# Sixteen DRAM copies of broadcast rows, a landing margin for more of a hand-written schedule, and two more products of ones

## The chip, the cores and the metric

The kernel runs on one core of a Trainium2 chip. Its time is the device time of one execution in microseconds (us), the median over the runs shown. The engines of the core are named as in the profile: PE is TensorE (PEld its weight loads), DVE is VectorE, ACT is ScalarE, POOL is GpSimd, SP is SyncE, which here issues nearly all of the DMAs. 16 DMA engines carry the transfers.

## The reference

One layer of a decoder trunk on 1024 tokens of 2048 channels, then a final RMSNorm, all in float32:

```python
h = rmsnorm(x, ln_g)
proj = h @ w_in                      # split into gMLP, DeltaNet and cross-attention columns
out_a = gmlp_spatial_gating(g_u, g_v, ws, bs, ln_g, ln_b) * silu(g_z)     # chunks of 128 tokens
q, k, v = split(silu(causal_conv(d_q, d_k, d_v)))                         # 8 heads of 128
g = -exp(a_log) * softplus(d_a + dt_bias); beta = sigmoid(d_b)            # decay and step per token and head
o = gated_delta_rule(l2norm(q), l2norm(k), v, g, beta)                    # chunks of 64 tokens, a scan over them
out_b = rmsnorm(o, dn_norm_g) * silu(d_z)
mk, mv = split(rmsnorm(mem, mem_norm_g) @ w_mem_kv)                       # 256 memory tokens
out_c = softmax(c_q @ mk.T / sqrt(128)) @ mv * silu(c_z)                  # 4 heads of 128
y = rmsnorm(x + concat(out_a, out_b, out_c) @ w_out, final_g)
```

Two things of it matter below. The vector `ln_g` (2048 values) multiplies every row of `x`, and so has to stand on all 128 partitions. The decays of a head, summed up over a chunk (a row of 512 values for each head and half of the tokens), have to stand on all partitions too, where the matrix of decays is made from them.

## The kernel before, in words

**Products.** Every large product is done as three products of float32 values that are split into a high and a low part (`whi`, `wlo` for weights, `ahi`, `alo` or `gt`, `inv` for the left side): ACT copies the high part, DVE subtracts it from the raw value. PE takes high x high, high x low and low x high into a PSUM bank (`acc` for the main sums, `dn` for the rest). The large projections go by a scheme with seven products of half blocks.

**The order of the work.** The program doesn't issue instructions as it states them. A class `Plan` records every operation with its engine, its dependencies and a rank (`rank(2)` around a block of the code: smaller goes first), gives it a cost, and then plays the program through: on each engine the next operation is the one of the smallest rank among those that are ready. When all have a planned start, they are sorted by it and issued, all from line 297, which is why the profile shows the one line L297 for everything and tells groups apart by tile names. No engine waits for the plan itself; only the order of each engine's instructions comes from it. When the plan decides at what time a successor `s` of a finished operation is ready, it adds a margin `s.late` to the end of a DMA (`o.moves`), or to the end of another engine's work that PE reads:

```python
o.late = self.slow if eng == "pe" else self.late if self.cls > self.URGENT else 0.0
...
if o.moves or s.eng == "pe" != e:
    when += s.late
```

So an operation that isn't PE's and has a rank above 2 is planned `late` nanoseconds after a load that it reads has landed. `late` is 0 until line 1235, which stands behind the first stage, and 1000 from there on. PE's own margin `slow` is 0 but for the two-head solves inside `levels` (800 there). The margin is in the plan alone: no instruction of the chip waits for it.

**The first stage.** PE starts with seven products of a matrix of ones with itself, `warm(7)` (each float32 product shows as two records), which go to a spare `dn` bank and are read by nobody. Then it transposes the first 512 columns of the 256 memory rows (`spread_mem(0)`, tiles `kT` and `qT` into `gt` and `inv`), and a loop over 16 steps `k` multiplies the 128 weight rows of step `k` (`load_kv`, tiles `ut` for the first four and `wraw`, loaded by SP) with the memory columns. The high part of the weights, `whi<-ut,gcol` or `whi<-wraw,gcol`, is made on ACT, which multiplies by the norm's weight on the way. In between stand the other column blocks of the memory (`spread_mem`) and the first token tiles of `x`: `load_x` brings 128 tokens in four blocks of 512 columns (tile `vs` for the first tile of tokens, `kd` for the second), `prep` squares them on ACT (`jk<-kd`), multiplies each by its scale and by `ln_g` on DVE, lets PE transpose the block into a spare bank and ACT empty that bank (`tn<-dn`). Each of these spare banks is one of two that take turns.

`ln_g` comes into four `zg` tiles, one for each 512 columns, each 128 partitions x 512 values. At step 3 of the loop SP issues four loads, and every one of them reads a single row of 2 KB in DRAM 128 times:

```python
if k == 3:
    with rank(2), behind(kvmark[-1]):
        for c in range(4):
            Q.dma_start(gb[c], ln_g[0, c * HT : (c + 1) * HT].partition_broadcast(P))
```

**The decays.** `decays` (line 785) makes the summed decays of one half of the tokens for all heads, transposes them into a tile `gr` of 64 rows x 128 and stores it to a DRAM tensor `gcd` of 8 heads x 512 (line 835). For each head and half, `qk` (line 922) loads the head's row on all partitions into a tile `E` through POOL's queue (line 936), again one row of 2 KB read 128 times, 16 loads in all. ACT makes exponentials of it.

**The later stages** are the projections, the two-head solves and scans of the gated delta rule (`front`, `inverse`, `levels`, `back`), the gating by chunks, the attention and the output projection. Most loaded tiles are split or copied by ACT and DVE before PE sees them. In a few places PE reads a loaded tile itself: the blocks of the two-head solves, the transposes of the first stage, and `gmlp` (line 1605), where SP loads `vd` into a tile `el` and PE multiplies it with `wsT`.

Of the kernel before, what the change touches and what calls it, by code (L numbers as in the profile page):

```python
# [17 lines left out]
P = 128  # L18
D = 2048
# [3 lines left out]
HT = 512  # L23
# [22 lines left out]

class Op:
    __slots__ = ("eng", "fn", "args", "kw", "cls", "idx", "cost", "lat", "moves", "lock", "n", "succ", "ready", "at",
                 "lead", "tail", "table", "late")


class Engine:
# [8 lines left out]
class Plan:  # L61
# [7 lines left out]
    TABLES = {AF.Exp: "exp", AF.Silu: "silu", AF.Gelu_apprx_tanh: "gelu"}  # L69
    TABLE_LOAD = 1500.0  # L70
    STAY = 1.5
    URGENT, LATE = 2.0, 1000.0

    def __init__(self, nc):
        self.ops = []
        self.seen = {}
        self.heir = {}
        self.users = {}
        self.cls = 5.0
        self.gate = None  # L80
        self.bundle = None
        self.late = self.slow = 0.0
        self.pe = Engine(self, "pe", nc.tensor)
        self.act = Engine(self, "act", nc.scalar)
        self.dve = Engine(self, "dve", nc.vector)
        self.pool = Engine(self, "pool", nc.gpsimd)
        self.sp = Engine(self, "sp", nc.sync)
# [50 lines left out]
    def add(self, eng, name, fn, args, kw):  # L138
        o = Op()
        o.eng, o.fn, o.args, o.kw, o.cls, o.idx = eng, fn, args, kw, self.cls, len(self.ops)  # L140
        o.succ, o.n, o.ready = [], 0, 0.0
        o.table = self.TABLES.get(args[2]) if eng == "act" and len(args) > 2 else None
        outs, ins = [], []
        for i, a in enumerate(args):
            if hasattr(a, "tensor"):
                (outs if i == 0 else ins).append(a)
        for key, a in kw.items():
            if hasattr(a, "tensor"):
                (outs if key in ("out", "accum_out") else ins).append(a)
        self.price(o, name, outs, ins)  # L150
        deps = set()
        if self.gate is not None:
            deps.add(self.gate)
        for write, aps in ((False, ins), (True, outs)):
            for ap in aps:
                key, p0, p1, mask = self.region(ap)
                log = self.seen.setdefault(key, [])
                keep = []
                for e in log:
                    q0, q1, m, w, op = e  # L160
                    if p0 < q1 and q0 < p1 and mask & m:
                        if (write or w) and op is not o:
                            deps.add(op)
                        if write and p0 <= q0 and q1 <= p1 and not m & ~mask:
                            continue
                    keep.append(e)
                keep.append((p0, p1, mask, write, o))
                self.seen[key] = keep
                if key in self.users:
                    self.users[key].append(o)  # L170
                    if write:
                        deps.update(self.users.get(self.heir.get(key), ()))
        o.lead, o.tail = o, []
        o.late = self.slow if eng == "pe" else self.late if self.cls > self.URGENT else 0.0
        if eng == "pe" and self.bundle is not None:
            if self.bundle:
                o.lead = self.bundle[0]
                o.lead.tail.append(o)
            self.bundle.append(o)
        for d in deps:  # L180
            if d.lead is not o.lead and o.lead not in d.succ:
                d.succ.append(o.lead)
                o.lead.n += 1
        self.ops.append(o)
        return o
# [42 lines left out]
    def issue(self):  # L228
        free = dict.fromkeys(self.SEEN, 0.0)
        soon = {e: [] for e in free}  # L230
        now = {e: [] for e in free}
        held = {"dve": 0.0, "pool": 0.0}
        dma = 0.0
        beside = dict.fromkeys(free, 0.0)
        table = "exp"
        for o in self.ops:
            if o.n == 0 and o.lead is o:
                heapq.heappush(soon[o.eng], (0.0, o.idx))
        left = len(self.ops)
        while left:  # L240
            best = None
            for e in free:
                if now[e]:
                    t = free[e]
                elif soon[e]:
                    t = max(free[e], soon[e][0][0])
                else:
                    continue
                if best is None or t < best[0]:
                    best = (t, e)  # L250
            t, e = best
            while soon[e] and soon[e][0][0] <= t:
                i = heapq.heappop(soon[e])[1]
                heapq.heappush(now[e], (self.ops[i].cls, i))
            if e == "act":
                other = [(c + self.STAY * (self.ops[i].table not in (None, table)), i, c) for c, i in now[e]]
                _, i, c = min(other)
                now[e].remove((c, i))
                heapq.heapify(now[e])
                head = self.ops[i]  # L260
            else:
                head = self.ops[heapq.heappop(now[e])[1]]
            for o in (head, *head.tail):
                t = max(t, free[e])
                if o.table not in (None, table):
                    t, table = t + self.TABLE_LOAD, o.table
                o.at = t
                left -= 1
                if o.lock:
                    t = max(t, held["pool" if e == "dve" else "dve"])  # L270
                end = t + o.cost
                if o.lock:
                    held[e] = end
                free[e] = end - min(self.OVERLAP[e], 0.5 * o.cost)
                done = end + o.lat
                if o.moves:
                    dma = max(dma, end) + o.moves
                    beside[e] = max(beside[e], end) + 2 * o.moves
                    done = (dma if e == "sp" else beside[e]) + self.DMA_FIXED + o.lat
                for s in o.succ:  # L280
                    if s.eng != e or o.moves:
                        when = done + self.SEEN[s.eng] + (self.SLACK if s.eng == "pe" else 0.0)
                    elif e == "pe":
                        when = free[e]
                    else:
                        when = end + 34.0
                    if o.moves or s.eng == "pe" != e:
                        when += s.late
                    s.ready = max(s.ready, when)
                    s.n -= 1  # L290
                    if s.n == 0:
                        heapq.heappush(soon[s.eng], (s.ready, s.idx))
            if len(head.tail) > 7:
                free[e] += self.SWITCH
        self.ops.sort(key=lambda o: (o.at, o.idx))
        for o in self.ops:
            o.fn(*o.args, **o.kw)  # L297
# [3 lines left out]
def kernel(  # L301
# [28 lines left out]
    R = Plan(nc)  # L330
# [90 lines left out]
    def tpb():  # L421
        turn["tp"] += 1
        return acc[2 + turn["tp"] % 2]

    h0_d = DT([KT, P, HT], "h0d")
    hT_d = DT([KT, P, HT], "hTd")

# [57 lines left out]
    def row_tiles(tag):  # L485
        if tag in ("inv", "gt", "ut"):
            return [b[:, i * HT : (i + 1) * HT] for b in (ring[tag](), ring[tag]()) for i in range(2)]
        return [ring[tag]() for _ in range(4)]

    gb = [ring["zg"]() for _ in range(4)]  # L490
    kvraw += [ring["ut"]() for _ in range(2)]
    mem_rows = [row_tiles("kT"), row_tiles("qT")]
# [20 lines left out]
    y1 = C([P, 2 * NT, 32], "y1")  # L513
    rows = y1.rearrange("p c m -> p (c m)")[:, 0:P]
    mrow = rows[0:16]
    with rank(2):
        load_mem(0)
        S.dma_start(mrow, mem_norm_g[0].rearrange("(c p) -> c p", p=P))
        for k in range(4):
            load_kv(k)  # L520
            if k == 1:
                load_mem(1)
    with rank(3):
        load_mem(2)
        load_mem(3)
# [66 lines left out]
    rm = []  # L592
    kvmark = []
    mhl = [spread_mem(0)]
    for k in range(KT):
        mh, ml = mhl[k // 4]
        if k >= 4:
# [16 lines left out]
        if k == 3:  # L614
            with rank(2), behind(kvmark[-1]):
                for c in range(4):
                    Q.dma_start(gb[c], ln_g[0, c * HT : (c + 1) * HT].partition_broadcast(P))
        if k in (1, 4, 8):
            with behind(kvmark[-1]):
                mhl.append(spread_mem(len(mhl)))  # L620
# [153 lines left out]
    r3, ww = ([steps[:, i * P : (i + 1) * P] for i in two] for two in ((0, 1), (2, 3)))  # L774
    scs = [C([P, 7, NT, NH], f"sc{hf}") for hf in range(2)]
    sct = C([P, 5, NT, NH], "sct")
    gcs = [DT([NH, HT], f"gcd{hf}") for hf in range(2)]
    scan_banks, work = dnr.bufs[0:2], over(dnr.bufs[2:4])

    def decay_mm(a, k):  # L780
# [4 lines left out]
    def decays(hf, a):  # L785
# [12 lines left out]
        with rank(1):  # L798
# [33 lines left out]
            V.tensor_copy(byh.rearrange("p (h t) -> p t h", t=NT), dp[:, 0:NU].rearrange("p (t h) -> p t h", h=NH))  # L832
            PE.transpose(tp[0:NU, 0:P], byh, ident)
            V.tensor_copy(gr, tp[0:NU, 0:P])
            Q.dma_start(gcs[hf].rearrange("h (t p) -> (h t) p", p=P), gr)


    todo = []
# [83 lines left out]
    def qk(h, hf, q, k, hs, gt):  # L922
# [10 lines left out]
        er = ring["E"]()  # L933
        e = tok(er)
        with behind(begun.get((h, hf))):
            G.dma_start(er, gcs[hf][h].partition_broadcast(P))
        vs = tok(ring["vs"]())
        S.activation(vs, e, AF.Exp)
        G.affine_select(out=e, in_=e, compare_op=ALU.is_ge, fill=NEG, base=0,
# [292 lines left out]
        decay_mm(a, k)  # L1232
    marks.append(R.ops[-1])
    decays(0, a)
    R.late = R.LATE
    todo += [lambda i=i: prep1(i) for i in range(NT)]
    todo += [lambda j=j: [*(whole(k) for k in range(j, KT, NJ)), left_sums(j)] for j in range(NJ)]
    gdrs = [front(0, 0, (first, None)), front(1, 0)]
# [580 lines left out]
```

## Time and profile before

| what | value |
|---|---|
| runs | 1626.97, 1629.0 and 1629.74 us, median 1629.0 us |
| profiled execution, its own time | 1630.94 us |
| its span on the chip | 1629.2 us, mean granted TensorE clock 0.998 |
| PE busy | 1611.6 us, 99% of the span |
| DVE, ACT, POOL busy | 77%, 63%, 18% |
| DRAM read, written | 339.57 MB, 87.06 MB: 262 GB/s over the span |

The rows in the next sections come from this one profiled execution. A row of the timeline gives the start, the length, the engine, the operation as `out<-in` with the tiles' names, and in brackets the idle time of the engine before it and what ended it. PEclk in a row of stretches is the granted TensorE clock, 1.00 being full. The stretches' DMA share is that of 16 engines, and can pass 1 where the records of packets overlap. An idle time of an engine costs something only if PE waits in the end.

### The profile page before, as it was taken

The numbers are of one execution on the slowest core, as the hardware profiler recorded it, in microseconds if no ns is written. First come the engines' busy times: TensorE is split into PE (matmuls) and PEld (weight loads), VectorE is DVE, ScalarE is ACT, GpSimd is POOL, SyncE is SP. The second block draws the span as 40 slices with busy tenths as digits, with TensorE's granted clock in tenths as the row PEclk, the third lists the DMA queues.
The fourth block names the chain that finished last, engine by engine and source line by source line (L and its number), as shares of the span: only waits on it lengthen the run. The fifth ranks groups of instructions, "written<-read, shape, count | busy, mean of one in ns | idle before, by whom it ended". The sixth has DMA issues, their size and how long they took to land.

```text
span 1629.2 us, 26133 instructions
## 1 busy us (share of the span) xinstructions
PE 1611.6 (99%) x8576; PEld 1354.8 (83%) x8576; DVE 1262.2 (77%) x2100; ACT 1027.0 (63%) x2217; POOL 300.3 (18%) x482
## 2 busy tenths in 40 slices
PE   8999999999999999999999999999999999999997
PEld 8988888888888888888888788888888888888886
DVE  5966787879756567899988897768768888789775
ACT  6767675765475457888685346766666775344355
POOL 0101220351452010225235005330100000000001
PEclk9999999999999999999999999999999999999999
DMA  9867898988977785689878977878968869688646
GB/s 309 241 179 225 280 301 251 278 282 309 359 257 242 261 283 190 204 286 368 281 243 253 320 228 241 266 265 296 319 201 274 282 218 364 207 273 293 218 146 239
DMA packets 277227, 428.94 MB, mean 263 GB/s; under 512 B 31017, under 2 KB 102242, under 8 KB 277090
## 3 DMA queue, kind: packets, MB, share of 16 engines
q1 hardware_dynamic: 254338, 366.81, 68.7%
q0 software_dynamic: 22144, 59.40, 10.9%
q8 instruction: 67, 1.10, 0.3%
q10 hardware_dynamic: 608, 1.06, 0.2%
q14 instruction: 70, 0.57, 0.1%
HBM read 339.57 MB, written 87.06 MB: 262 GB/s over the span
## 4 chain that ended last, share of the span: by engine, by line
PE 89%; DMA 6%; DVE 2%; issue 1%; ACT 1%; SPq 1%; POOLq 0%; POOL 0%; DVEq 0%; ACTq 0%
PE acc L297 69%; PE dn L297 20%; DMA wraw<-in_w_in_dram 1%; SPq L297 1%; DMA vs<-od 1%; DMA kT<-in_mem_dram 1%; DVE alo L297 0%; DMA wraw<-hTd 0%; DVE y L297 0%; DMA ai<-in_w_in_dram 0%; DMA kd<-in_x_dram 0%; DMA y<-in_w_in_dram 0%; DMA wraw<-in_w_out_dram 0%; DMA pd<-y 0%; DMA wraw<-in_w_mem_kv_dram 0%
## 5 line engine op out<-in xcount | busy, mean ns | idle before, releaser
L297 PE MATMUL acc<-ahi,whi 128*128 128x512 f32 (+1 forms) x1512 | 535.5, 392 | 0.0
L297 PE MATMUL acc<-ahi,wlo 128*128 128x512 f32 (+1 forms) x1144 | 446.9, 391 | 0.0
L297 PEld LDWEIGHTS acc<-ahi,whi 128*128 128x128 f32 x1512 | 283.2, 188 | 53.9
L297 PE MATMUL acc<-alo,whi 128*128 128x512 f32 (+1 forms) x776 | 302.1, 389 | 0.2 <-DVE alo L297 0.2
L297 PEld LDWEIGHTS acc<-ahi,wlo 128*128 128x128 f32 x1144 | 215.2, 188 | 41.0 <-DVE wlo L297 0.4
L297 ACT CAST whi<-wraw 128x512 fp32r<-128x512 f32 (+1 forms) x167 | 134.2, 804 | 129.1 <-PE acc L297 86.7
L297 DVE TENSOR_TENSOR wlo<-wraw,whi 128x512 fp32r<-128x512 f32 (+1 forms) x167 | 154.0, 922 | 60.7 <-ACT whi L297 56.9
L297 ACT CAST ahi<-raws 128x1024 fp32r<-128x1024 f32 x130 | 136.3, 1049 | 61.2 <-PE acc L297 26.9
L297 PEld LDWEIGHTS acc<-alo,whi 128*128 128x128 f32 x776 | 146.0, 188 | 27.6 <-DVE alo L297 0.6
L297 PE MATMUL acc<-ahi,zl 128*128 128x512 f32 x376 | 148.2, 394 | 0.0
L297 PE MATMUL acc<-alo,zh 128*128 128x512 f32 x376 | 148.2, 394 | 0.0
L297 PE MATMUL acc<-ahi,zh 128*128 128x512 f32 x376 | 148.1, 394 | 0.0
L297 POOL TENSOR_TENSOR small<-small,mhalf 128x1 f32<-128x1 f32 x26 | 18.0, 696 | 590.9 <-DVE small L297 578.0
L297 DVE TENSOR_TENSOR alo<-raws,ahi 128x1024 fp32r<-128x1024 f32 x65 | 79.3, 1220 | 19.7 <-ACT ahi L297 19.5
L297 DVE TENSOR_TENSOR ahi<-raws,ahi 128x1024 fp32r<-128x1024 f32 x65 | 79.2, 1219 | 18.2 <-ACT ahi L297 17.9
L297 DVE TENSOR_TENSOR alo<-y,ahi 128x1024 fp32r<-128x1024 f32 x65 | 79.2, 1219 | 15.7 <-ACT ahi L297 15.4
L297 ACT CAST ahi<-y 128x1024 fp32r<-128x1024 f32 x65 | 68.1, 1048 | 35.1 <-PE dn L297 19.2
L297 PEld LDWEIGHTS acc<-ahi,zl 128*128 128x128 f32 x376 | 70.7, 188 | 13.8
L297 PEld LDWEIGHTS acc<-ahi,zh 128*128 128x128 f32 x376 | 70.7, 188 | 13.8
L297 PEld LDWEIGHTS acc<-alo,zh 128*128 128x128 f32 x376 | 70.7, 188 | 13.8
L297 PE MATMUL acc<-whi,ahi 128*128 128x512 f32 x232 | 79.7, 391 | 0.0
L297 PE MATMUL dn<-whi,ahi 128*128 128x512 f32 x216 | 74.1, 389 | 0.0
(422 smaller groups left out, 3414.3 us busy)
## 6 DMA issues: line engine op xcount, KB each, us to landing
wraw<-in_w_in_dram SPq DMA_DIRECT2D x268, 256.0 KB, 4.0
raws<-sd SPq DMA_DIRECT2D x150, 256.0 KB, 4.1
y<-in_w_in_dram SPq DMA_DIRECT2D x92, 256.0 KB, 4.7
y<-sd SPq DMA_DIRECT2D x75, 256.0 KB, 3.6
wraw<-in_w_out_dram SPq DMA_DIRECT2D x64, 256.0 KB, 4.7
raws<-h0d SPq DMA_DIRECT2D x54, 256.0 KB, 5.1
y<-in_w_out_dram SPq DMA_DIRECT2D x33, 256.0 KB, 4.8
sd<-zg SPq DMA_DIRECT2D x32, 256.0 KB, 4.0
```

Source lines behind the costliest of these rows:

```text
L297: o.fn(*o.args, **o.kw)
```

## The change

There are four edits.

1. `ln_g` is first written 16 times to a new DRAM tensor `lngd` (16 rows of 2048), by one more DMA of SP after the second weight block. The four `zg` loads then read from it: the 128 partitions take the 16 copies in turn, eight times over, instead of one row 128 times. The decays' store writes 16 copies as well, and each `E` load reads its head's 16 copies in turn.
2. A margin `FIRST` of 1000 ns stands from the first tile of the first stage on, so that operations of ACT, DVE, POOL and SP with a rank above 2 are planned 1 us behind a load that they depend on there too. Behind the first stage the value is `LATE`, as before.
3. A new margin `land` of 1000 ns is added for PE operations that depend on a DMA directly. It is 0 in the first stage and stands from line 1235 on (1243 in the changed kernel).
4. `warm(2)`: two more products of ones, stated between `spread_mem(0)` and the first weight products.

The margins are again in the plan alone. Because the whole program is issued in the plan's order, edits 1 to 3 can move instructions on every engine.

```diff
-    URGENT, LATE = 2.0, 1000.0
+    URGENT, LATE, FIRST = 2.0, 1000.0, 1000.0
...
+        o.land = self.land
         o.late = self.slow if eng == "pe" else self.late if self.cls > self.URGENT else 0.0
...
                     if o.moves or s.eng == "pe" != e:
                         when += s.late
+                    if o.moves and s.eng == "pe":
+                        when += s.land
...
+    COPIES = 16
...
+    R.late = R.FIRST
     gb = [ring["zg"]() for _ in range(4)]
...
+    lng_d = DT([COPIES, D], "lngd")
     with rank(2):
         load_mem(0)
...
             load_kv(k)
             if k == 1:
                 load_mem(1)
+                Q.dma_start(lng_d, ln_g[0].partition_broadcast(COPIES))
...
     mhl = [spread_mem(0)]
+    warm(2)
     for k in range(KT):
...
                 for c in range(4):
-                    Q.dma_start(gb[c], ln_g[0, c * HT : (c + 1) * HT].partition_broadcast(P))
+                    Q.dma_start(gb[c], lng_d[:, c * HT : (c + 1) * HT].partition_broadcast(P // COPIES))
...
-    gcs = [DT([NH, HT], f"gcd{hf}") for hf in range(2)]
+    gcs = [DT([COPIES, NH, HT], f"gcd{hf}") for hf in range(2)]
...
-            Q.dma_start(gcs[hf].rearrange("h (t p) -> (h t) p", p=P), gr)
+            Q.dma_start(gcs[hf].rearrange("r h (t p) -> (h t) r p", p=P), rep(gr, COPIES))
...
-            G.dma_start(er, gcs[hf][h].partition_broadcast(P))
+            G.dma_start(er, gcs[hf][:, h].partition_broadcast(P // COPIES))
...
     decays(0, a)
-    R.late = R.LATE
+    R.late = R.land = R.LATE
```

More of the change, by code (lines that the diff above doesn't have):

```diff
@@ L48 @@
     __slots__ = ("eng", "fn", "args", "kw", "cls", "idx", "cost", "lat", "moves", "lock", "n", "succ", "ready", "at",
-                 "lead", "tail", "table", "late")
+                 "lead", "tail", "table", "late", "land")
 class Engine:
@@ L81, in __init__ @@
         self.bundle = None
-        self.late = self.slow = 0.0
+        self.late = self.slow = self.land = 0.0
         self.pe = Engine(self, "pe", nc.tensor)
```

## The prediction

> **What bounds the kernel now.** I read the page first, then the waits of TensorE, then the timeline around the longest of them. The page says that PE is the bound nearly everywhere:
>
> ```profile
> PE 1611.6 (99%) x8576; PEld 1354.8 (83%) x8576; DVE 1262.2 (77%) x2100; ACT 1027.0 (63%) x2217; POOL 300.3 (18%) x482
> PE 89%; DMA 6%; DVE 2%; issue 1%; ACT 1%; SPq 1%; POOLq 0%; POOL 0%; DVEq 0%; ACTq 0%
> ```
>
> PE is busy in 1611.6 of 1629.2 us, and the diff takes no product away. So the change can only win back what PE waits, or what it runs at less than full clock. The waits of PE (waiter, releaser, us in total, times, longest):
>
> ```profile
> PE dn L297 <- ACT tn L297: 1.9, 1, 1.9
> PE dn L297 <- DMA el<-vd: 1.7, 1, 1.7
> PE dn L297 <- POOL ones L297: 1.1, 1, 1.1
> PE acc L297 <- ACT gt L297: 0.9, 1, 0.9
> PE dn L297 <- ACT vs L297: 0.9, 1, 0.9
> PE dn L297 <- ACT E L297: 0.6, 1, 0.6
> PE dn L297 <- POOL gt L297: 0.4, 1, 0.4
> ```
>
> The first lies in the first stage. The timeline of ACT there (start, us, what, idle before it in brackets):
>
> ```profile
> 28.34 1.15 ACT L297 ACTIVATE whi<-ut,gcol 128x1024 fp32r<-128x1024 f32 x1 [0.33 <-PE dn L297]
> 33.83 0.63 ACT L297 ACTIVATE jk<-kd 128x512 bf16<-128x512 f32 x1 [4.34 <-DMA kd<-in_x_dram]
> 34.46 1.13 ACT L297 ACTIVATE whi<-wraw,gcol 128x1024 fp32r<-128x1024 f32 x1
> 36.11 0.56 ACT L297 COPY tn<-dn 128x512 f32<-128x512 f32 x1
> ```
>
> ACT stands 4.34 us on the square of the second token tile (jk<-kd) until that row block lands; behind it are queued the hi part of a weight block and, at 36.11, the copy that empties a PSUM bank. PE needs that bank. The timeline of PE, and the stretches around it (length, PE, PEld, DVE, ACT, POOL busy, PEclk, DMA share, GB/s):
>
> ```profile
> 36.73 0.66 PE L297 MATMUL dn<-ident,vs 128*128 128x128 f32 x4 [1.93 <-ACT tn L297]
> 37.58 0.28 PE L297 MATMUL acc<-gt,whi 128*128 128x256 f32 x1
> 39.54 0.41 PE L297 MATMUL acc<-gt,whi 128*128 128x256 f32 x1
> ...
> 25.00:27.00 2.00, 2.00 (x19) 1.95 (x18) 1.10 (x2) 2.00 (x5) 0.00 (x0) 1.00 0.83 210
> 27.00:29.00 2.00, 2.00 (x14) 1.77 (x13) 1.69 (x4) 1.67 (x4) 0.00 (x0) 1.00 0.86 197
> 33.00:35.00 2.00, 1.80 (x11) 1.20 (x9) 0.00 (x0) 1.17 (x3) 0.00 (x0) 1.00 1.06 418
> 35.00:37.00 2.00, 0.27 (x2) 0.27 (x3) 1.37 (x2) 2.00 (x5) 0.00 (x0) 1.00 1.01 412
> 37.00:39.00 2.00, 2.00 (x15) 2.00 (x14) 1.25 (x2) 2.00 (x6) 0.00 (x0) 0.70 1.12 268
> 39.00:41.00 2.00, 2.00 (x9) 1.82 (x9) 1.38 (x4) 2.00 (x5) 0.00 (x0) 0.50 0.82 237
> 41.00:43.00 2.00, 2.00 (x13) 1.70 (x12) 1.72 (x3) 1.17 (x2) 0.00 (x0) 0.95 0.95 269
> ```
>
> The idle time is 1.93 us, and right after it the granted clock falls to half: the same product takes 0.41 us at 39.54 where it took 0.28 at 37.58. The clock's share is lost over three stretches: 2 x (0.30 + 0.50 + 0.05) = 1.70 us. This one late row block so costs 1.93 + 1.70 = 3.63 us. The Trainium skill, page TensorE: Matmul & The Clock Gate, section "Why this matters for your kernels", wants PE gaps over about 3 us before the clock falls; here 1.93 us of idle was enough, and the measurement decides. By that rule the 1.70 us would not hang on this wait, and only 1.93 us could be had.
>
> **Part 1: spread rows of ln_g, and their place on SP.** The row block is late because of what stands ahead of it:
>
> ```profile
> 22.21 0.33 SPq L297 DMA_DIRECT2D wraw<-in_w_mem_kv_dram  x1
> 22.59 2.49 SPq L297 DMA_DIRECT2D zg<-in_ln_g_dram  x4
> 25.18 0.38 SPq L297 DMA_DIRECT2D wraw<-in_w_mem_kv_dram  x1
> 25.59 3.63 SPq L297 DMA_DIRECT2D kd<-in_x_dram  x4
> ```
>
> The four zg loads each read one 2 KB row 128 times. While they run, the engines move 210 and 197 GB/s, against 418 and 412 once they are through. Four times 256 KB are 1.05 MB: 5.15 us at the mean of the first pair, 2.53 at the mean of the second. If 16 copies take the whole difference away, kd lands 2.6 us earlier; if none, 0. Slow stretches of 237 GB/s stand at 39 to 41 us without any such load, which speaks against the whole. Second, in the changed program's order SP issues the zg loads ahead of the first wraw and the first kd ahead of the second wraw. That is 512 KB less ahead of kd: 0.52 MB at 415 GB/s, 1.26 us. Together up to 3.9 us of ACT's 4.34. PE's wait is gone from 1.93 on, so half of the first gain is enough beside the second; I take all of the 3.63 us (ends: 0, and -3.63). What is late next is the weight block wraw, now behind the four zg loads; its hi part stands behind jk<-kd on ACT as before, so it has the time of that square.
>
> Ahead of this SP writes the copies, one DMA more of 16 rows of 8 KB, issued about 20 us before its reader. One issue is 0.33 us on SP by the row at 22.21; nobody waits then, since the loads queued behind it are used late: 0, and 0.33 us if that cover were gone.
>
> **Part 2: the margin of the first stage (FIRST).** It moves only instructions of a rank above 2 behind a DMA: squares, stores, small loads. In the changed order the square jk<-kd still stands ahead of whi<-wraw on ACT, so the knot above is not untied by it. One square of the memory rows moves behind two copies, and one whi moves ahead of them. I take 0, bounded by one wait of the list either way: 0.9.
>
> **Part 3: the margin for TensorE's reads (land).** It makes the planner place a PE instruction 1 us later behind a load that it reads itself. The trace has one PE wait of this kind (the third line is a stretch):
>
> ```profile
> 920.12 0.70 SPq L297 DMA_DIRECT2D el<-vd  x1
> 925.71 1.13 PE L297 MATMUL dn<-wsT,el 128*128 128x128 f32 x8 [1.68 <-DMA el<-vd]
> ...
> 920.00:960.00 40.00, 38.32 (x177) 31.75 (x176) 36.09 (x64) 16.58 (x19) 0.55 (x1) 1.00 0.78 263
> ```
>
> One us more of products ahead leaves 0.7 of 1.68: -1.0 (ends: 0 and -1.68). The clock stayed at 1.00 in that stretch, so nothing hangs on this wait. The margin also reorders PE from about 430 us on, where the two-head solves read loaded tiles. The waits there, 0.9 <- ACT vs and 0.4 <- POOL gt, are on engines and not on loads; they will be dealt anew. I take 0 for them, bounded by -1.3 (both gone) and +1.3 (two more of their kind).
>
> **Part 4: two more products of ones.** They go between the first transposes and the first weight products:
>
> ```profile
> 1.05 3.36 PE L297 MATMUL dn<-ones 128*128 128x128 f32 x14 [1.05 <-POOL ones L297]
> 6.51 0.69 DVE L297 TENSOR_TENSOR inv<-dn,gt 128x512 fp32r<-128x512 f32 x1 [1.67 <-ACT gt L297]
> 7.62 1.22 PE L297 MATMUL acc<-gt,whi 128*128 128x256 f32 x4 [0.92 <-ACT gt L297]
> 10.14 0.41 PE L297 MATMUL acc<-gt,wlo 128*128 128x256 f32 x1
> 10.53 0.28 PE L297 MATMUL acc<-gt,wlo 128*128 128x256 f32 x1
> ```
>
> Seven products are 14 records in 3.36 us, so two take 0.96. They write a bank that DVE has read by 7.20 at the earliest, so they end at 8.16, where the first weight product stood at 7.62: +0.54. PE runs at half clock until about 10.4 (0.41 against 0.28); if the filled gap lets the clock open earlier, half of the 2.8 us from 7.62 comes back, -1.4. No row shows that it would, so I take +0.54.
>
> **Part 5: spread rows of the decays.** The store gcd<-gr grows 16 times, to 256 KB, and 16 loads of E read the copies:
>
> ```profile
> E<-gcd POOLq DMA_DIRECT2D x16, 256.0 KB, 6.7
> kT<-late POOLq DMA_DIRECT2D x16, 256.0 KB, 4.8
> ```
>
> An E takes 1.9 us longer to land than a plain load of the same queue and size. No PE wait in the list is on E's load, so up to 16 x 1.9 us of transfers are hidden: 0. If that cover were gone on the other side (copies that land later), each late E could cost PE its lateness; that is in the second rival.
>
> **Sum.** -3.63 - 1.0 + 0.54 = -4.1 us. The profiled execution took 1630.94 us with a span of 1629.2, so it would come to 1626.8; the median of the runs is 1629.0, 1.9 below it, so the forecast is 1624.9. A measurement of this kernel tells about 0.2% (3.3 us) from no change.
>
> **Rivals.**
> Half the engines, at full rate. The load of the copies has 8 as its slowest source dimension (8 repeats over 16 rows). The mechanism: a load cut into 8 equal parts runs on 8 of the 16 engines. Half of 415 GB/s is 207 GB/s, what the four loads get now, so they take 5.05 us as before and only the 1.26 us of the order are won. PE's wait shrinks to 0.67; the 1.68 us of idle at 925 us did not cost the clock, so the 1.70 go too: -1.26 - 1.70 - 1.0 + 0.54 = -3.4, 1625.6 us. For it: the shapes; against it: no load of this size in the trace is cut so. Chance 0.23. The Trainium skill states this rule, page DMA: Bandwidth & Descriptors, section "Rules for kernel authors": a leading repeat of c copies, with c below 16, keeps a whole DMA on at most c engines. No run here shows it yet.
>
> Half the engines, and still slowed (slower than before). If those 8 engines also keep today's rate each, 102 GB/s, the four loads take 10.3 us, 5.15 longer, less 1.26 for the order. kd is 3.9 us later and so is PE: +3.9 - 1.0 + 0.54 = +3.4, 1632.4 us; a late E, cut the same way, adds to it. It decides from the point at which the four loads take over 5.15 + 1.26 = 6.4 us. For it: the 8 engines walk the same 16 rows in the same order, so they can still meet on one row. Chance 0.22.
>
> No effect. The slow stretch is not the repeated row (237 GB/s at 39 us has none), kd lands as late as now, and what the margin wins at 925 us the added products and one new wait of 0.4 give back: 1629.0 us. Chance 0.10.
>
> **How the numbers follow.** Forecast 0.45, rivals 0.23, 0.22 and 0.10. The forecast's own ends: with all of el's wait, both bounded waits and the earlier clock, -3.63 - 1.68 - 1.3 - 1.4 = -8.0, 1621.0; the runs of before differ by 2.8 us, half of which I add: 1620. Upward the range takes in the slow rival: 1632.5. Faster by over 0.2%: 0.85 of the forecast and half of the first rival, 0.50. Slower: nine tenths of the second rival, 0.20. The rest is 0.30.
>
> **What would show it.** Right: no wait of ACT over 2 us on kd; no row PE dn <- ACT tn; PEclk at 1.00 from 37 to 43 us; over 300 GB/s from 23 to 29 us; el's wait under 1 us. The first rival: zg loads land 1.2 us apart at about 200 GB/s, a PE wait of 0.7. The second: kd lands after 36 us, PE idle over 4 us near 36. Wrong altogether: a new PE wait over 2 us outside the first stage, most likely behind E or in the solves from 430 us on.

## The result, and the profile after

The changed kernel takes 1640.37 us (median of 4 runs, 1637.21 to 1643.51) where the kernel before takes 1627.99 (median of 4, one more than in the table above): a ratio of 1.0077, with a 95% interval from 1.0056 to 1.0098. It is slower by some 12 us. 1624.9 was forecast, and the range ended at 1632.5.

The profiled execution took 1637.21 us with a span of 1635.5, 6.3 us more than before's. It is the shortest of the four (1637.21, 1637.43, 1643.31 and 1643.51), so it shows only half of the 12 us. The busy line and the chain of its page:

```profile
PE 1614.0 (99%) x8580; PEld 1356.0 (83%) x8580; DVE 1261.0 (77%) x2100; ACT 1021.4 (62%) x2213; POOL 291.9 (18%) x482
PE 86%; DMA 6%; issue 3%; DVE 2%; ACT 1%; SPq 0%; POOL 0%; POOLq 0%; DVEq 0%; ACTq 0%
```

PE is still the bound, with 2.4 us more of busy time, of which the added products explain 1; the other 3.9 of the 6.3 us are waiting. The waits of PE (waiter, releaser, us in total, times, longest) say where:

```profile
PE dn L300 <- DMA el<-vd: 3.1, 1, 3.1
PE dn L300 <- POOL gt L300: 2.1, 1, 2.1
PE dn L300 <- ACT ahi L300: 1.4, 1, 1.4
PE acc L300 <- ACT whi L300: 1.4, 1, 1.4
PE dn L300 <- DVE ai L300: 1.1, 1, 1.1
PE dn L300 <- ACT tn L300: 0.9, 1, 0.9
```

The wait on el grew from 1.7 to 3.1, that on POOL's gt from 0.4 to 2.1, and those on ahi and ai are new or larger. The wait on tn has fallen from 1.9 to 0.9, but one of 1.4 on whi stands just before it. Three places are looked at here.

**The first stage.** ACT's and PE's timelines (start, us, what, idle before it), and the stretches (PE, PEld, DVE, ACT, POOL busy, PEclk, DMA share, GB/s):

```profile
33.10 0.63 ACT L300 ACTIVATE jk<-kd 128x512 bf16<-128x512 f32 x1 [4.88 <-DMA kd<-in_x_dram]
```

```profile
34.92 0.39 PE L300 MATMUL acc<-gt,whi 128*128 128x256 f32 x1 [1.38 <-ACT whi L300]
36.23 0.66 PE L300 MATMUL dn<-ident,vs 128*128 128x128 f32 x4 [0.93 <-ACT tn L300]
```

```profile
25.00:27.00 2.00, 2.00 (x14) 1.72 (x13) 2.00 (x3) 1.95 (x6) 0.00 (x0) 1.00 1.04 273
27.00:29.00 2.00, 2.00 (x17) 1.86 (x16) 1.13 (x4) 1.15 (x1) 0.55 (x1) 1.00 1.05 258
29.00:31.00 2.00, 2.00 (x16) 1.86 (x15) 2.00 (x4) 0.00 (x0) 0.00 (x0) 1.00 1.04 271
...
37.00:39.00 2.00, 2.00 (x12) 2.00 (x11) 0.86 (x2) 1.93 (x5) 0.00 (x0) 0.50 0.96 313
```

The row block kd lands only 0.7 us earlier than before, although SP issued it earlier and the copies were there; the engines move 258 to 273 GB/s, and the clock still falls after PE's waits. PE is idle for 4.1 us of the first 60 here and for 4.2 before, so in this execution the first stage neither wins nor loses. It was a mild case. The runs e3 and e4 below have the same first stage, with the same order on every engine, and there PE waits longer on whi (e3, then e4):

```profile
PE acc L300 <- ACT whi L300: 3.3, 1, 3.3
```

```profile
PE acc L300 <- ACT whi L300: 5.5, 2, 5.2
```

That such longer waits are the other half of the 12 us is likely, but no trace of a run near 1643 us shows it.

**The first two-head solve.** POOL's timeline and PE's (after), then POOL's of before:

```profile
450.91 1.24 POOL L300 DMA_DIRECT2D E<-gcd  x2
453.66 1.15 POOL L300 DMA_DIRECT2D tblk<-tdrearly  x2 [1.51 <-DMA ut<-udrearly]
454.80 0.69 POOL L300 MEMSET gt<- 64x256 f32 x2
```

```profile
455.54 1.10 PE L300 MATMUL dn<-tblk,gt 128*128 128x64 f32 x8 [2.14 <-POOL gt L300]
```

```profile
438.35 0.69 POOL L297 MEMSET gt<- 64x256 f32 x2
...
443.26 0.55 POOL L297 DMA_DIRECT2D E<-gcd  x1
```

Before, the solve's last loads and the clearing of gt came first and E after them. In the changed order two E loads stand ahead of them in POOL's queue, and the solve stands 16 us later.

**The load el.** SP's line, PE's, and the stretch behind:

```profile
928.28 0.43 SPq L300 DMA_DIRECT2D el<-vd  x1
```

```profile
933.43 1.13 PE L300 MATMUL dn<-wsT,el 128*128 128x128 f32 x8 [3.06 <-DMA el<-vd]
```

```profile
456.00:460.00 4.00, 4.00 (x15) 3.27 (x15) 1.77 (x3) 0.73 (x2) 2.22 (x4) 0.60 0.98 216
934.00:938.00 4.00, 4.00 (x16) 3.22 (x15) 3.15 (x5) 0.00 (x0) 0.00 (x0) 0.59 1.06 398
```

PE has nothing left to do at 933.43 - 3.06 = 930.37, 2.1 us after SP issued el; before, it was 3.9 us. After this wait and the one at 455.54 PE runs at half clock for 3.4 us each, which costs 1.7 us each time. These two places, with the waits on ahi and ai, are where this execution loses against before's.

### The profile page after: what moved, and what is told of

Its sections match the earlier page's. It is cut to its first block, busy times and chain, and to the rows that moved or that the text cites. A ratio compares the mean times of both kernels' runs of the same rounds, so it can differ in the third digit from the quotient of the medians.

```text
span 1635.5 us, 26123 instructions
## 1 busy us (share of the span) xinstructions
PE 1614.0 (99%) x8580; PEld 1356.0 (83%) x8580; DVE 1261.0 (77%) x2100; ACT 1021.4 (62%) x2213; POOL 291.9 (18%) x482
## 4 chain that ended last, share of the span: by engine, by line
PE 86%; DMA 6%; issue 3%; DVE 2%; ACT 1%; SPq 0%; POOL 0%; POOLq 0%; DVEq 0%; ACTq 0%
PE acc L300 66%; PE dn L300 21%; DMA ut<-in_w_mem_kv_dram 1%; DMA wraw<-in_w_in_dram 1%; DMA y<-in_w_in_dram 1%; DMA gd<-y 1%; DMA kd<-in_x_dram 1%; DMA gt<-gt 0%; DVE wlo L300 0%; DMA tdrearly<-inv 0%; SPq L300 0%; DMA wraw<-hTd 0%; DVE y L300 0%; DMA raws<-h0d 0%; DMA tblk<-tdrearly 0%
```

## The experiments

Theory A, formed from this profile, put the whole loss into the order; its rival B into the copies. Two edits separate them, because the plan sees the copies only through the price of the store: a store can be made sixteenfold and priced as one, or the other way round. All medians stand beside the kernel before on the same chip.

| run | what it is | us | before | ratio (95%) |
|---|---|---|---|---|
| e1 | copies, order of before | 1640.38 | 1626.48 | 1.0082 (1.0068 to 1.0097) |
| e2 | order of after, no copies | 1631.55 | 1626.48 | 1.0032 (1.0021 to 1.0044) |
| e3 | after without land | 1643.01 | 1626.48 | 1.0104 (1.0089 to 1.0118) |
| e4 | after without the decays' copies | 1633.32 | 1626.48 | 1.0047 (1.0034 to 1.0061) |
| e5 | FIRST and the two products | 1624.49 | 1627.24 | 0.9984 (0.9975 to 0.9994) |
| e6 | e5, ln_g: 16 rows, 8 repeats outside | 1633.00 | 1627.24 | 1.0037 (1.0026 to 1.0049) |
| e7 | e5, ln_g: 16 rows outside, 8 repeats inside | 1627.11 | 1627.24 | 1.0002 (0.9993 to 1.0010) |
| e8 | e5 in the order of the dearer store | 1635.36 | 1627.24 | 1.0053 (1.0037 to 1.0069) |
| e9 | e5, ln_g: one row, 8 x 16 repeats | 1631.22 | 1627.04 | 1.0020 (1.0011 to 1.0028) |
| e10 | FIRST alone | 1624.83 | 1627.04 | 0.9984 (0.9975 to 0.9992) |
| e11 | e5 and land | 1628.03 | 1627.04 | 0.9998 (0.9988 to 1.0008) |
| e12 | the decays' copies, order of before | 1631.25 | 1627.04 | 1.0027 (1.0018 to 1.0035) |
| e13 | e5, ln_g: first copy, 128 repeats | 1625.14 | 1627.25 | 0.9989 (0.9980 to 0.9998) |
| e14 | e7 with the rows 2 KB apart | 1626.65 | 1627.25 | 1.0001 (0.9990 to 1.0012) |
| e15 | e8, margin of 5 us for PE's reads of el | 1629.77 | 1627.25 | 1.0014 (1.0005 to 1.0022) |
| e16 | e5, ln_g: one row, 16 x 8 repeats | 1627.39 | 1627.01 | 0.9999 (0.9989 to 1.0009) |

### Copies or order: e1 to e4

e1, against after (no margins, no added products); e2, against after, with the zg and E loads of before (the copies of ln_g are still stored, but not read):

```diff
-                Q.dma_start(lng_d, ln_g[0].partition_broadcast(COPIES))
+                o = Q.dma_start(lng_d, ln_g[0].partition_broadcast(COPIES))
+                o.cost = o.moves = 0.0
...
-            Q.dma_start(gcs[hf].rearrange(...), rep(gr, COPIES))
+            Q.dma_start(gcs[hf].rearrange(...), rep(gr, COPIES)).moves /= COPIES
```

```diff
-            Q.dma_start(gcs[hf].rearrange(...), rep(gr, COPIES))
+            Q.dma_start(gcs[hf].rearrange("h (t p) -> (h t) p", p=P), gr).moves *= COPIES
```

> The copies of ln_g and of the decays are stored and read as in the changed kernel, but they are priced in the plan as one row was, and margins and added products are left out: every engine's order is that of before. Theory A (the loss is in the order): within 2 us of before, 1626 to 1630. Theory B (copies read by 8 engines, or their stores, slow the rest): 1634 to 1641, as the changed kernel.

> The order of the changed kernel on every engine, kept by pricing the store as sixteen rows, but the loads read one row 128 times again and the decays' store writes one copy. Theory A: 1636 to 1643, with PE's waits on gt near 455 us and on el near 930 us still there. Theory B: 1626 to 1630.

e3 and e4 undo one part of after each (`R.late = R.LATE` without land; the decays' store and loads of before).

> The changed kernel without the margin for PE's reads. In the order POOL's two loads of E then stand behind the second pair of tblk loads and the clearing of gt near 440 to 455 us. Theory A1 (the margin and the copies' price together put E ahead of tblk): the 2.1 us wait of PE on gt falls under 0.7, and the time is 1629 to 1634. Theory A2 (the copies' price alone loses the time): 1636 to 1641.

> The changed kernel without the copies of the decays. E stands behind tblk as before. Theory A1: wait on gt under 0.7, 1626 to 1632. Theory A3 (the margin for PE's reads alone loses the time, by reordering from 430 us on): 1635 to 1641.

Theory A fell at once: with the order of before the copies still cost 13.9 us. Its longest wait stands in the first stage, where PE waits for ACT's copy out of the spare bank and the clock is then at half for 6.8 us; a second one, of 3.8 us on DVE's states, ends near 456 us. The first:

```profile
PE dn L300 <- ACT tn L300: 5.5, 1, 5.5
```

But B alone isn't right either, for the new order without copies costs 5.1 us, between the two forecast ranges. e2 also shows a gain hidden under this: its PE has no wait near 35 us, and its el wait is the largest seen, 4.0 us. Theory A1 had the place right, for in e3 E stands behind the clearing of gt again and the wait on gt is gone from the list; but the time doesn't fall, so this wait isn't where the loss lies. e4 lies between the ranges of A1 and A3; its waits on gt and el are gone, and its first stage has the longest wait on whi. By the waits of PE, el is late by over 3 us in after, e2 and e3, and not in e1 and e4: it goes with the price that the plan puts on the decays' store, not with land.

### What the first stage's order gives, and what ln_g's copies cost: e5, e6, e7, e10

```diff
-                    Q.dma_start(gb[c], lng_d[:, c * HT : (c + 1) * HT].partition_broadcast(P // COPIES))
+                    Q.dma_start(gb[c], rep(lng_d[:, c * HT : (c + 1) * HT], P // COPIES)).lat = 3500.0
```

This is e7 against e6; the price is set to that of e6, so the order is the same. e5 has the load of before there and no store; e10 also leaves `warm(2)` out.

> Only FIRST and the two products of ones; rows are read as before, and the order behind the first stage is that of before. Theory C (the first stage's new order takes away the wait on kd, as in the run without copies, which was 5 us ahead at 35 us): 1620 to 1623.5, no PE wait over 1 us between 25 and 45 us. Rival D (that run was lucky): a wait of 1.5 us or more there, 1624.5 to 1628.

> As the last, with the sixteen copies of ln_g read as in the changed kernel (8 repeats outside, 16 rows inside). Theory E (8 engines carry each load): under 220 GB/s for 8 us or more from about 23 us, PE waits 3 to 6 us near 35 us, 1624 to 1632. Rival (the copies cost nothing): as the last kernel.

> As the last, but the loads walk the 16 copies outside and the 8 repeats inside; order and bytes are the same. Theory E (the number of engines decides): over 350 GB/s while they run, no PE wait over 1 us near 35 us, 1620 to 1624. Rival F (the copies themselves, their store or place in DRAM, are slow): as the kernel with 8 outside, 1624 to 1632.

> FIRST alone, without the two products. If the whole gain is FIRST's order: 1623 to 1625.5. If the two products carry part of it by opening the clock earlier: 1625.5 to 1627.5.

e5 is 0.16% below the kernel before, just clear of the noise, with PE busy without a break from 17 to 45 us; the time lies between the ranges of C and D. SP's timeline and the stretches of e5:

```profile
16.54 0.33 SPq L300 DMA_DIRECT2D ut<-in_w_mem_kv_dram  x1
16.91 4.24 SPq L300 DMA_DIRECT2D zg<-in_ln_g_dram  x4
21.55 0.33 SPq L300 DMA_DIRECT2D wraw<-in_w_mem_kv_dram  x1
22.18 0.33 SPq L300 DMA_DIRECT2D kd<-in_x_dram  x1
```

```profile
23.00:25.00 2.00, 2.00 (x20) 2.00 (x19) 1.11 (x4) 1.99 (x5) 0.00 (x0) 1.00 1.12 390
25.00:27.00 2.00, 2.00 (x14) 1.72 (x13) 1.97 (x5) 1.76 (x6) 0.00 (x0) 1.00 0.97 387
27.00:29.00 2.00, 2.00 (x15) 1.82 (x15) 1.04 (x2) 1.02 (x2) 0.55 (x1) 1.00 1.04 414
```

The same four loads of one row, 128 times each, are issued from 16.91 where they stood at 22.59, behind a wraw that SP didn't issue before 22.21. The last of them has landed by 26.8 us, so they run at 390 and 387 GB/s, a plain load's rate: one repeated row isn't slow. Nor does the order of before make it slow. e12 below has the first stage of before, with the same order on every engine, and its stretches are:

```profile
25.00:27.00 2.00, 2.00 (x16) 1.91 (x16) 1.29 (x2) 2.00 (x5) 0.00 (x0) 1.00 0.71 235
27.00:29.00 2.00, 2.00 (x14) 1.77 (x14) 1.50 (x3) 1.70 (x4) 0.30 (x1) 1.00 1.02 336
29.00:31.00 2.00, 2.00 (x14) 1.78 (x13) 1.86 (x2) 0.11 (x1) 0.25 (x1) 1.00 1.03 390
```

The engines had less to move in the slowest of these (a DMA share of 0.71), and the first three of its four loads land 0.6 and 0.7 us apart, where those of before's profiled execution land 2.1 and 0.9 us apart. PE's wait on tn is 0.60 us there, not 1.93, and the clock stays at 1.00. So the slow stretch, and part of the 3.63 us, belonged to one execution. In that execution the packets of 2 KB took a median of 84 ns from 25 to 29 us, as elsewhere, but 28 of 369 packets took over 300 ns, up to 1.6 us, and the DMA share was 0.83 and 0.86. What held them up stays open.

e10 gives the same ratio without the two products, so the gain is FIRST's, and the products give nothing that these runs can tell.

e6 reads the copies as the change does. Its stretches:

```profile
23.00:25.00 2.00, 2.00 (x17) 1.82 (x16) 1.25 (x3) 1.97 (x6) 0.00 (x0) 1.00 1.02 225
25.00:27.00 2.00, 2.00 (x14) 1.78 (x13) 1.98 (x3) 1.97 (x5) 0.00 (x0) 1.00 1.03 227
27.00:29.00 2.00, 2.00 (x16) 1.90 (x15) 1.09 (x4) 1.48 (x3) 0.55 (x1) 1.00 1.06 237
29.00:31.00 2.00, 2.00 (x14) 1.77 (x13) 2.00 (x3) 0.00 (x0) 0.00 (x0) 1.00 1.07 235
```

Eight us at 225 to 237 GB/s, then PE waits 3.34 us near 37 us and the clock is at half for 6.8 us: 8.5 us behind e5. The wait is that of theory E, the time is 1 us above its range. The wait in the list:

```profile
PE acc L300 <- ACT whi L300: 3.3, 1, 3.3
```

e7, with 16 rows outside, has 250 to 280 GB/s for 6 us and loses 2.6 us, so 16 engines alone don't bring e5's time back.

### The number of engines, or the copies: e9, e13, e14, e16

Each changes the source of the four loads alone, in the order of e5 or e6:

```diff
+ e9   ln_g[0, c * HT : (c + 1) * HT].partition_broadcast(16).partition_broadcast(8)
+ e16  ln_g[0, c * HT : (c + 1) * HT].partition_broadcast(8).partition_broadcast(16)
+ e13  lng_d[0, c * HT : (c + 1) * HT].partition_broadcast(P)
+ e14  rep(lng_d[c], P // COPIES)      # lng_d is [4, COPIES, HT] here
```

> FIRST and the two products; ln_g is read from its one row, no copies, but the loads' source is written as 8 repeats of 16 repeats. Theory J (8 engines make the load slow): about 200 to 240 GB/s while the four loads run, packets of 2 KB well over 84 ns, PE waits 2 us or more near 35 us, 1628 to 1633. Theory K (8 engines at full rate, the copies' addresses make packets long): packets at 84 ns, about 210 GB/s for 5 us, 1624 to 1628. Rival (the outer dimension doesn't matter): loads 0.65 us apart, 1622 to 1626.

> FIRST, the two products and the store of the sixteen copies of ln_g, but each load reads only the first copy 128 times, outermost, so that 16 engines carry it. If several rows make packets long (theory M): loads 0.65 to 0.70 us apart, packets of 2 KB at 84 ns, 1623 to 1626. If the freshly written DRAM tensor is slow to read (theory N): loads about 1.04 us apart, 1625.5 to 1629, as with 16 rows.

> As the kernel that walks 16 copies outside, but the copies of one column block stand 2 KB apart in DRAM, not 8 KB. If the distance of the rows makes packets long (theory M1): loads 0.65 to 0.75 us apart, 1623 to 1626. If the distance doesn't matter (M2, or N): 1.0 us apart, 1625.5 to 1629.

> FIRST and the two products; ln_g is read from its one row, no copies, with the loads' source written as 16 repeats of 8 repeats, so that 16 engines carry each load. If the two-level form of the source makes packets long (theory P): loads 1.0 to 1.1 us apart, packets of 2 KB at 125 to 140 ns, 1625.5 to 1629. If several rows do (theory M): 0.65 to 0.70 us apart, 84 ns, 1623 to 1626.

The queue's packets on the page (number, MB, share) tell the engines. e5, e16 and e9, one line each:

```profile
q1 hardware_dynamic: 254338, 366.81, 68.6%
```

```profile
q1 hardware_dynamic: 254338, 366.81, 68.8%
```

```profile
q1 hardware_dynamic: 254306, 366.81, 68.8%
```

e9 moves the same bytes in 32 packets fewer, all of them of 4 bytes: 8 for each of its four loads, as if 8 of 16 engines sent no closing packet. e16, with 16 repeats outside, has as many as e5, and e6 has 32 fewer than e7 in the same way (254338 and 254370). So a source with 8 outside runs on 8 engines, copies or not. That is the rule of the Trainium skill, page DMA: Bandwidth & Descriptors, section "Rules for kernel authors", which the prediction had weighed as a rival; the traces agree.

The rest is something else. The issues of the zg loads (KB each, median us to landing) of e5, e7 and e16:

```profile
zg<-in_ln_g_dram SPq DMA_DIRECT2D x4, 256.0 KB, 6.7
```

```profile
zg<-lngd SPq DMA_DIRECT2D x4, 256.0 KB, 8.2
```

```profile
zg<-in_ln_g_dram SPq DMA_DIRECT2D x4, 256.0 KB, 8.9
```

One row with a source in two levels (e16) is as slow as sixteen rows in two levels (e7), also where the rows lie 2 KB apart (e14); one copy read in a single level (e13) is as fast as the input itself. In the landing times the loads of e5 and e13 are 0.64 to 0.67 us apart and those of e7, e14 and e16 1.0 to 1.5 us, and the latter's packets of 2 KB take a median of 121 to 141 ns from 23 to 27 us, where those of e5 take 84 to 87. Theories M and N fell, P holds: the two-level form makes the load slow, not the rows, their distance or the new tensor. Why the form does so stays open. With 8 outside the time is longer again (e9 against e16, 0.21%), and that sixteen rows are slower there than one (e6 against e9, 0.17%) is at the edge of the noise.

### The order of the dearer store: e8, e15; margin and decays alone: e11, e12

> FIRST and the two products, with the plan's order that the sixteen-fold store of the decays brings, but one copy stored and read; the margin for PE's reads is left out. Theory G (the order that this price brings makes el late): PE waits over 2.5 us for el near 925 us and the clock falls behind it, 5 to 7 us behind the kernel with FIRST and the products alone, 1625.5 to 1630. Rival (the margin or the copies make it late): wait under 2 us, 1620 to 1624.

> FIRST, the two products and the order of the sixteen-fold store's price, no copies, with a margin of 5 us in the plan for PE's products of el alone. If el's lateness is what that order costs (theory G): no PE wait on el over 0.5 us and 1628 to 1631.5, about 5 us below the kernel without this margin (1635.4). If the cost lies in many re-dealt waits instead: 1633 to 1637.

e8 is e5 with the `.moves *= COPIES` of e2. e15 adds a margin around the products of `gmlp` alone:

```diff
+        R.land = 5000.0
         for tt in range(NT):
             PE.matmul(hand[:, tt * P : (tt + 1) * P], vg[:, tt], wsT[g], start=True, stop=True)
+        R.land = 0.0
```

PE's timeline of e8:

```profile
928.31 0.91 PE L300 MATMUL dn<-wsT,el 128*128 128x128 f32 x6 [3.83 <-DMA el<-vd]
```

SP issues el 1.5 us before PE runs out of other work here, and 5.8 us before it in e5. Nothing but the order differs between e5 and e8, and the order's only cause is a price in the plan: 10.9 us by the medians, 5.7 between the two profiled executions. That is more than theory G's range, and the clock didn't fall behind the wait on el, as G had it. With the margin on el (e15) this wait is gone and the time falls by 5.6 us, inside G's range; since the margin also changes what stands behind it, that the wait alone is worth 5.6 us isn't shown. The other 5.3 us weren't taken apart; e15's waits name ut<-udrearly with 2.0 us and E with 1.8.

> FIRST, the two products and the margin for PE's reads, no copies. Theory L (the margin re-deals small waits and gains nothing in the order without the sixteen-fold store's price; the sums give 0.3 us): 1623 to 1627. If the margin works as meant, el's wait of 0.3 us and those of the two-head solves go: 1620 to 1623.

> The copies of the decays stored and read, nothing else; the store is priced as one row, so every engine's order is that of before. Theory H (the E loads are hidden): 1625.5 to 1629. Theory I (E's loads by 8 engines come late, a part of the 14 us that both copies cost in the old order): 1630 to 1634, with PE, through ACT or DVE, waiting behind E near 440 us.

e11: the margin for PE's reads gains nothing in the order of before (0.9998 against e5's 0.9984, a loss at the edge of the noise and above both forecast ranges), while in the order of the dearer store it takes off 0.21% (e2 against e8) and 0.27% (after against e3). Whether it helps hangs on the order. e12: the copies of the decays cost 0.27% where the order stays. Their loads of E take 7.6 us to landing, where before's take 6.7:

```profile
E<-gcd POOLq DMA_DIRECT2D x16, 256.0 KB, 7.6
```

The time is in theory I's range. PE waits 2.16 us near 448 us there, on DVE's states. That E's lateness makes this wait is not shown: e6, which has no copies of the decays, waits 2.73 us on DVE's states near 454 us.

**The sum.** By the ratios: FIRST -0.16%, the copies of ln_g +0.53% (e6 against e5), the dearer store's order +0.69% (e8 against e5), land in that order -0.21%: +0.85%. Measured were +0.77%, so reading the decays' copies adds nothing visible in the new order. Each of these figures is uncertain by 0.1 to 0.2%, so the 0.27% that e12 shows for them in the old order isn't excluded.

## Why the prediction was wrong, step by step

- **Part 1, the copies.** The step that failed is "if 16 copies take the whole difference away, kd lands 2.6 us earlier; if none, 0". The slow stretch of one execution was read as the mark of a repeated row. It wasn't: e5 reads the same row at 387 GB/s and more, and e12 reads it in the order of before with loads 0.6 to 0.7 us apart. And the term ended at 0, as if the copies could cost nothing: they cost 8.5 us (e6 against e5, 0.53%), most of it by the way in which the loads are written: one row read as 8 x 16 costs 0.36% (e9 against e5).
- **Part 1, the order on SP.** Right in sign, too small: 1.26 us were taken for less bytes ahead of kd. In e5 the loads start 5.7 us earlier, ACT's square no longer waits for kd, PE doesn't wait there and the clock stays at 1.00. By time that is -0.16%, about 2.6 us, for the 3.63 of the sum, which rested on the one slow execution. The gain belonged to FIRST, which part 2 had put at 0.
- **The second rival** had the first stage right, with 0.22: 8 engines, each still slow, ten us for four loads. e6 is 6 us slower than before, where the rival had 3.4; it left the clock's loss as before, while e6 has 6.8 us at half clock, 1.7 us more lost. The first rival's full rate on 8 engines was not seen.
- **Part 3, land.** -1.0 was wrong for the changed kernel: the wait on el became 3.06. The margin isn't its cause (e3 has 3.5 without it); the price of the store is. The margin did take off some 0.2 to 0.3% in that order, more than the 1.0 us, but not by ending el's wait, and by which waits isn't shown.
- **Part 4, the products.** +0.54 was forecast; e5 and e10 have the same ratio, each within 0.1% (1.6 us) either way, which can't tell 0.54 from 0.
- **Part 5, the decays.** "Up to 16 x 1.9 us of transfers are hidden: 0" is the largest miss of a term. It costed the transfers and not the price that the plan puts on the store. That price moved the first solve by 16 us (POOL's clearing of gt stands at 434.72 in e5 and at 450.90 in e8) and made el late in SP's queue: 0.69%. Together with land it also put E ahead of the solve's loads in POOL's queue (in after and e2, not in e3 and e8). The bounds for new waits, 0.9 and 1.3 us, came from the waits that one good order had left; another order has others. The text named such a wait "behind E or in the solves from 430 us on" as what would prove it wrong, and gave it no chance.
- **The clock.** That 1.93 us of idle can cost 1.7 us more was borne out: see below.

## What to carry to other kernels

Before a load's rate is blamed on its addresses, look whether a second execution shows it, whether the engines were busy (the DMA share) and when the queue issued it: here an earlier place in SP's queue took PE's waits near 35 us away without any copies. Write a broadcast source in one level with the largest count outside; splitting it into 8 x 16 halved the engines and slowed the packets. In a planned schedule a changed price is a change of the whole program: separate it from the transfer itself by pricing the new as the old, and don't bound the waits of a new order by those of a tuned one.

## What the runs showed of the hardware that was not expected

While four broadcast loads with a source in two levels run, the engines move 241 to 294 GB/s, though 16 of them carry each load (e16); with the same bytes in one level they move 387 to 390 (e5).

PE's clock falls to half in pieces of 3.4 us (or two of them, 6.8, in e1, e4, e6 and e9), and whether a wait brings one is not told by its length: in e10 the clock fell after a wait of 1.11 us near 452 us, in e7 after one of 1.62, and behind the 3.83 us at 928 us in e8 it did not. The first two stand among products of 64 and 128 columns in the two-head solves; whether the work around a wait decides wasn't tested. The stretch behind each, of e10 and of e8:

```profile
453.00:457.00 4.00, 4.00 (x14) 3.36 (x14) 4.00 (x8) 2.82 (x7) 2.23 (x4) 0.57 0.31 92
```

```profile
930.00:934.00 4.00, 4.00 (x23) 3.47 (x22) 3.81 (x7) 0.00 (x0) 0.00 (x0) 1.00 0.94 330
```

Without the one at the program's end there is one such piece before, three in after and none in e5. The Trainium skill, page TensorE: Matmul & The Clock Gate, section "Why this matters for your kernels", takes gaps over about 3 us for the limit; it falls here after much shorter gaps too, and a longer one passed without.
